# A weight ring of nine double slots and one spare slot in place of nineteen single slots

## The chip, the core and the metric

The kernel runs on one core of a Trainium2 chip. The metric is the device time of the program in microseconds (us); below it stands as the median of three runs. Float32 is used throughout.

## What is computed

A batch of one, T = 256 tokens, width D = 1024, goes through three layers. Layers 0 and 1 have a modulation from a condition vector, layer 2 has none:

```python
cond = silu(c)
for layer in range(2):                              # layers 0 and 1
    shift1, scale1, gate1, shift2, scale2, gate2 = split(cond @ ada_w[layer] + ada_b[layer], 6)
    h = rms(x, norm1_w[layer]) * (1 + scale1) + shift1
    y = even_mixer(h) if layer == 0 else odd_mixer(h)
    x = x + gate1 * y
    h = rms(x, norm2_w[layer]) * (1 + scale2) + shift2
    x = x + gate2 * hier_moe(h, w1, w3, w2)
h = rms(x, attn_norm_2); x = x + second_mixer(h)    # layer 2
x = x + hier_moe(rms(x, ffn_norm_2), w_gate, w_up, w_down)
return rms(x, final_norm_2)
```

The even mixer is a sliding-window attention beside a gated linear attention, the odd mixer a causal attention of 8 heads, the second one a sparse attention (compressed, selected and window branches) beside a linear recurrence, with gates that merge the two. Each mixer multiplies `h` by a wide input matrix and its result by an output matrix of 1024 x 1024. The MoE picks one of 4 groups and 2 of its 8 experts for each token; an expert is `(silu(t @ w1[e]) * (t @ w3[e])) @ w2[e]` with 512 hidden columns. So each of the 32 experts of a layer has three matrices of 2 MB (1024 x 512 twice, 512 x 1024 once), 192 MB a layer.

## The kernel before

All work is issued by one Python class, `Net`; the order of every engine's instructions is the order in which its methods emit them.

**The ring.** Big weights and the large buffers of the mixers share one pool of `RING` = 19 slots of 128 partitions x 2048 float32 (1 MB each, 8192 bytes a partition). `plan` (line 185) appends a transfer to a list: a key, the function that gives destination and source, and the shape. All of a program's transfers are planned at the start, in the order of their use: even mixer, MoE 0, odd mixer, MoE 1, second mixer, MoE 2. `pump` (line 188) takes transfers from the head of the list as long as the count `free` is above `reserve`, takes a slot of the ring for each and issues it on SyncE's queue (line 194). The count is kept in Python: it says how many slots the program order allows; on the chip SyncE waits at an issue until the slot's last readers are through. `get` returns a transfer that is issued, `done` gives its slot back and calls `release`, which raises `free` and pumps. `slot` takes a slot for a mixer's own buffer; `want` asks for one as soon as one is free; `reserve` keeps slots back for mixers' buffers that come later. For layer 2 a pool `extra` of two more slots, in space that the mixers have left, is used first (`more`).

**Mixers.** `plan_cols` (line 567) plans a slab of columns of an input matrix: 512 columns as two transfers of 1 MB (4 of 8 row groups each, 2048 bytes in a row), narrower slabs as one. `plan_rows` (line 574) plans half of an output matrix as two transfers of 512 columns. `plan_mod` (line 306) plans half of a modulation vector's matrix as two transfers with rows of 4 KB. Each chunk of two row groups of a slab is split into a rounded part and a rest by ScalarE, VectorE and GpSimd (`prep`, lines 461 to 463) into one of the mixer's split buffers `wbufs` (four slots; five in the second mixer, the fifth outside the ring); `prep` keeps at most one chunk fewer ready than there are buffers. `slab` then issues the matmuls of a chunk, each as three passes of the parts. The mixers' stages are interleaved by `weave`, a list of generators with written estimates of their times; beside them the modulation vectors are computed (`mods`, line 314) at places given by the lists `EVEN` and its like. A mixer ends with `out_last` (line 520), which takes `hT` (one slot, the turned tokens for the router) and `hs` (two slots, the tokens in two parts for the gather); `hs` stays through the MoE.

**MoE.** The 32 experts are handled in 16 pairs (`moe`, line 1791). A pair's tokens are gathered by matmuls into `xg`; `up` (line 1844) makes the gate pass and the up pass, `turn` transposes, `down` (line 1887) makes the down pass, `combine` adds the pair before into `x`. A pass alternates the two experts: each writes its 64 rows of the same result. The gate matrices of a pair are four transfers of 1 MB: `plan_moe` (line 1600) cuts every expert's matrix in halves, in the order expert 0 lower half, expert 1 lower half, expert 0 upper, expert 1 upper; each has rows of 8192 bytes a partition. `up` gives two slots back after its fourth row group and two at its end, `down` likewise after each half. The last pair's down matrices go in four slots of 256 columns of both experts (`down_last`, line 1910), so that the output can begin early. After pair 5 (`LATE`) an extra step serves tokens beyond an expert's 64 places. The numbers at the end of `moe`'s calls in `body` (line 2020; 8, 14, 0) are the slots that the last pair keeps back for the next mixer.

All matmuls of weights are at line 258 (`mm`), transposes at 268 (`tr`). Small operands are loaded on ScalarE's queue, `x` on SyncE's.

Of the kernel before, what the change touches and what calls it, by code (L numbers as in the profile page):

```python
# [9 lines left out]
FT = mybir.dt.float32  # L10
FR = mybir.dt.float32r
# [8 lines left out]
P = 128  # L20
# [9 lines left out]
RING = 19  # L30
# [92 lines left out]
class Net:  # L123
    def __init__(self, tc, ctx, A, out):
# [4 lines left out]
        self.ring = pool("ring", RING)  # L129
        self.ps = pool("ps", 8, space=PSUM)  # L130
# [35 lines left out]
    def outputs(self, c, key="out"):  # L166
        def use():
            s = self.slot(FR)
            self.o += [s[:, T * c * i:T * c * i + T * c].rearrange("p (c t) -> p c t", c=c) for i in range(SLOT // T // c)]
            self.flag((key, len(self.o)))  # L170
        self.want(use)
# [11 lines left out]
    def pump(self):  # L183
        while self.queue and (self.more or self.free > self.reserve):
            key, parts, (a, b) = self.queue.pop(0)
            if self.more:
                t = self.more.pop().tile([P, SLOT], FT, name="more", tag="more")
                self.mine.add(key)
            else:
                self.free -= 1  # L190
                t = self.ring.tile([P, SLOT], FT, name="slot", tag="slot")
# [122 lines left out]
    def mods(self, l, v, hs):  # L314
        p = self.psum()
        for h in hs:
            for j in range(2):
                w = self.get(("ada", l, v, h, j))
                for k in range(2):
                    for n in range(2):  # L320
                        q = slice(64 * n + 32 * k, 64 * n + 32 * k + 32)
                        self.mm(p[q], self.condz[:, 4 * h + 2 * j + k, 31 - v:63 - v], w[:, k, 512 * n:512 * n + 512],
                                h == hs[0] and not j, h == hs[-1] and j == 1)
                self.done(("ada", l, v, h, j))
# [98 lines left out]
    def begin_mixer(self, turned=None, mid=None):  # L423
# [4 lines left out]
        self.hh, self.hl = (self.slot(FR).rearrange("p (k q) -> p k q", k=KC) for i in range(2))  # L428
# [91 lines left out]
    def out_last(self, act, gate):  # L520
# [3 lines left out]
        self.hT = self.slot().rearrange("p (k q) -> p k q", k=KC)  # L524
        self.hs = [self.slot(FR).rearrange("p (t k q) -> p t k q", t=NT, k=KC) for i in range(2)]
# [41 lines left out]
    def plan_cols(self, key, w, c0, n):  # L567
        src = w.rearrange("(p k) n -> p k n", k=KC)[:, :, c0:c0 + n]
        m = KC if n * KC <= SLOT else 4
        for i in range(KC // m):  # L570
            self.plan((key, i), lambda t, i=i: [(t, src[:, m * i:m * i + m])], [m, n])
        self.chunks[key] = [((key, k // m), k % m, k % m == m - 2) for k in range(0, KC, 2)]

    def plan_rows(self, key, w, grouped=False):
        for i in range(2):
            ws = w[:, 512 * i:512 * i + 512]
            if grouped:
                src = ws.rearrange("(g r d) n -> g d r n", g=2, d=64)
                self.plan((key, i), lambda t, src=src: [(t[64 * g:64 * g + 64], src[g]) for g in range(2)], [4, 512])
            else:  # L580
                src = ws.rearrange("(k p) n -> p k n", p=P)
                self.plan((key, i), lambda t, src=src: [(t, src)], [4, 512])
        self.chunks[key] = [((key, i), k, k == 2) for i in range(2) for k in (0, 2)]
# [107 lines left out]
    def gla(self, g, q):  # L691
# [116 lines left out]
        self.release(4, reserve=3)  # L808
# [83 lines left out]
    def even(self, coeffs):  # L892
        nc = self.nc
        with self.tc.tile_pool(name="even", bufs=1, reuse_waits="tile") as g:
            setup = self.bias_setup(g)
            self.setup(lambda: next(setup))
            self.reserve = 10
# [8 lines left out]
            self.weights(["e_qa", "e_ka", "e_qb", "e_vb", "e_rb", "e_oa", "e_ob"], [self.slot(FR) for i in range(4)])  # L906
# [4 lines left out]
            bias, sc = (self.slot().rearrange("p (h s) -> p h s", h=8) for i in range(2))  # L911
            q = [self.slot() for i in range(2)]
# [31 lines left out]
            def stream():  # L944
                yield from self.slab_tm(512, s_qa)

                def use_att():
                    s = self.slot()
                    self.att, self.ob = s[:, :1024], s[:, 1024:]
                    self.flag("att", 0.7)  # L950

                def use_vb():
                    s = self.slot()
# [4 lines left out]
                self.want(use_vb)  # L958
# [1115 lines left out]
```

## Time and profile before

| | |
|---|---|
| median of three runs | 2072.07 us (2068.1 to 2073.53) |
| the profiled execution's own time | 2067.69 us |
| its span | 2065.9 us |
| mean granted TensorE clock | 0.974 |
| PE (matmul) busy | 1897.2 us, 92% |
| PEld (weight load) / DVE / ACT / POOL busy | 49% / 40% / 22% / 15% |
| moved by DMA | 725.29 MB, mean 351 GB/s |
| expert weights `slot<-moe_w` | 376 transfers of 1024 KB, 19.8 us from issue to landing |

Times are in us from the span's start. A row such as `ps<-slot,xg` names the written tile and the read ones; SPq is SyncE's queue of transfers. PEclk is the granted TensorE clock as a share of its full speed. Engines wait for each other and for transfers by semaphores; "<-" in brackets names what ended a wait. PE's matmuls follow each other in a pipeline, so a busy PE can be one that moves slowly through its queue.

### The profile page before, as it was taken

What the parts mean: (1) busy time and instruction counts of PE and PEld (TensorE: products, weight loads), DVE (VectorE), ACT (ScalarE), POOL (GpSimd) and SP (SyncE); (2) the same over time, 40 slices, a digit from 0 to 9 for tenths busy, and PEclk for the clock granted to TensorE, in tenths of its full rate; (3) what the DMA queues carried; (4) which work ended last, traced back from release to release, by engine and by line L of the source; (5) the groups of instructions that cost most, each with busy time, mean ns of one, the idle gap of its engine ahead of it and who ended that gap; (6) DMA issues with size and microseconds to landing.
All of it is one profiled execution on the core that took longest, in us unless ns stands there. A gap on an engine that the chain in (4) does not pass through costs nothing.

```text
span 2065.9 us, 25147 instructions
## 1 busy us (share of the span) xinstructions
PE 1897.2 (92%) x10032; PEld 1022.1 (49%) x10032; DVE 822.9 (40%) x1553; ACT 458.3 (22%) x838; POOL 309.8 (15%) x245
## 2 busy tenths in 40 slices
PE   6898999998989989999999889998899999999987
PEld 3655444343333657544433334586788443344333
DVE  3666433232322657623322222467666323222222
ACT  1424211111110443311111111254543111111111
POOL 1331000000000424000000000242443000000000
PEclk8998999999999999999999999999999999999999
DMA  8796999999999956799999999931357999999997
GB/s 314 274 312 251 375 422 421 420 421 422 421 420 405 367 211 242 303 401 421 421 421 421 421 421 421 342 106 42 131 191 268 379 421 421 420 421 421 421 421 287
DMA packets 157541, 725.29 MB, mean 351 GB/s; under 512 B 25305, under 2 KB 43087, under 8 KB 85225
## 3 DMA queue, kind: packets, MB, share of 16 engines
q1 hardware_dynamic: 139216, 716.84, 86.4%
q10 hardware_dynamic: 18201, 6.76, 1.3%
q8 instruction: 82, 1.34, 0.3%
q14 instruction: 42, 0.34, 0.0%
HBM read 722.48 MB, written 1.07 MB: 350 GB/s over the span
## 4 chain that ended last, share of the span: by engine, by line
DMA 23%; PE 19%; DVE 3%; issue 3%; ACT 2%; ACTq 0%; POOL 0%; POOLq 0%; SPq 0%; DVEq 0%
PE ps L258 18%; DMA slot<-moe_w 8%; DMA slot<-w_gate 5%; DMA slot<-w_up 4%; DMA slot<-w_down 2%; DMA more<-w_down 2%; DMA more<-w_up 2%; PE ps L268 1%; DVE slot L1287 1%; ACT slot L1275 1%; DMA slot<-w_in 0%; ACT slot L461 0%; DVE slot L462 0%; DVE hh L1861 0%; DVE wx L462 0%
## 5 line engine op out<-in xcount | busy, mean ns | idle before, releaser
L258 PE MATMUL ps<-slot,xg 128*64 128x512 f32 x2952 | 700.2, 599 | 47.5 <-DMA slot<-moe_w 34.3
L258 PEld LDWEIGHTS ps<-slot,xg 128*64 128x64 f32 x2952 | 225.0, 138 | 490.2 <-issue 381.2
L258 PE MATMUL ps<-slot 128*128 128x256 f32 (+8 forms) x2230 | 370.2, 327 | 11.5 <-DVE slot L462 9.0
L258 PE MATMUL ps<-slot,ht 128*64 128x512 f32 (+1 forms) x1592 | 341.7, 570 | 4.9 <-ACT ht L249 4.9
L258 PEld LDWEIGHTS ps<-slot 128*128 128x128 f32 (+3 forms) x2230 | 300.0, 186 | 72.2 <-issue 16.0
L1861 DVE SCALAR_TENSOR_TENSOR hh<-sg,ws,ps 128x512 f32<-128x512 f32 x48 | 54.3, 1130 | 603.6 <-PE ps L258 349.1
L258 PEld LDWEIGHTS ps<-slot,ht 128*64 128x64 f32 x1592 | 113.8, 137 | 198.1 <-issue 183.2
L1882 POOL TENSOR_TENSOR yl<-sg,yh 128x512 fp32r<-128x512 f32 (+1 forms) x68 | 82.4, 1211 | 862.5 <-ACT yh L1881 862.5
L463 POOL TENSOR_TENSOR slot<-slot 128x512 fp32r<-128x512 f32 (+2 forms) x108 | 163.5, 1531 | 279.5 <-ACT slot L461 247.3
L1908 DVE TENSOR_TENSOR x<-x,ps 128x512 f32<-128x512 f32 x180 | 113.6, 680 | 43.7 <-PE ps L258 41.5
L462 DVE TENSOR_TENSOR slot<-slot 128x512 fp32r<-128x512 f32 (+2 forms) x108 | 105.7, 992 | 57.3 <-ACT slot L461 54.6
L258 PEld LDWEIGHTS ps<-u,slot 128*128 128x128 f32 x864 | 105.6, 195 | 23.4 <-issue 17.0
L461 ACT CAST slot<-slot 128x1024 fp32r<-128x1024 f32 (+2 forms) x108 | 106.5, 1020 | 46.4 <-PE ps L258 24.8
L258 PE MATMUL ps<-u,slot 128*128 128x256 f32 (+1 forms) x864 | 111.0, 287 | 3.5 <-DVEq L1743 3.5
L1880 DVE TENSOR_TENSOR sg<-ps,ga 128x512 f32<-128x512 f32 (+1 forms) x68 | 44.9, 660 | 166.1 <-PE ps L258 155.8
L1857 ACT ACTIVATE sg<-ps 128x512 f32<-128x512 f32 x48 | 28.7, 597 | 325.7 <-PE ps L258 325.7
L1881 ACT CAST yh<-sg 128x512 fp32r<-128x512 f32 (+1 forms) x68 | 40.3, 593 | 251.7 <-DVE sg L1880 251.7
L258 PE MATMUL ps<-yh,pg 128*128 128x512 f32 (+1 forms) x204 | 85.5, 421 | 0.7 <-ACT yh L1881 0.7
L249 ACT COPY ht<-ps 128x512 f32<-128x512 f32 x48 | 28.1, 585 | 252.1 <-PE ps L268 251.9
L258 PE MATMUL ps<-yl,pg 128*128 128x512 f32 (+1 forms) x204 | 78.8, 389 | 4.3 <-POOL yl L1882 4.0
L399 ACT ACTIVATE xg<-ps,cf 128x256 f32<-128x256 f32 (+1 forms) x72 | 39.0, 542 | 172.6 <-PE ps L258 172.6
L1933 POOL TENSOR_TENSOR slot<-x,rows 128x512 f32<-128x512 f32 x2 | 2.6, 1276 | 460.2 <-DVE x L1929 460.2
(333 smaller groups left out, 1555.0 us busy)
## 6 DMA issues: line engine op xcount, KB each, us to landing
slot<-moe_w SPq DMA_DIRECT2D x376, 1024.0 KB, 19.8
slot<-w_gate SPq DMA_DIRECT2D x59, 1024.0 KB, 19.8
slot<-w_down SPq DMA_DIRECT2D x55, 1024.0 KB, 19.8
slot<-w_up SPq DMA_DIRECT2D x54, 1024.0 KB, 19.8
slot<-ada_w SPq DMA_DIRECT2D x48, 1024.0 KB, 9.0
slot<-w_in SPq DMA_DIRECT2D x20, 1024.0 KB, 7.4
slot<-odd_w_in SPq DMA_DIRECT2D x12, 1024.0 KB, 17.0
more<-w_up SPq DMA_DIRECT2D x10, 1024.0 KB, 16.1
```

The costliest lines, as they stand in the source:

```text
L249: self.nc.scalar.copy(out, in_)
L258: self.nc.tensor.matmul(out, lhsT=lhsT, rhs=rhs, start=start, stop=stop)
L399: self.nc.scalar.activation(out, p, AF.Identity, scale=a, bias=nb[:, k:k + 1])
L461: nc.scalar.copy(wh, src)
L462: nc.vector.tensor_sub(wl[:, 0], src[:, 0], wh[:, 0].bitcast(FT))
L463: nc.gpsimd.tensor_sub(wl[:, 1], src[:, 1], wh[:, 1].bitcast(FT))
L1857: nc.scalar.activation(sg, ps, AF.Silu)
L1861: nc.vector.scalar_tensor_tensor(ha.rearrange("s k p -> s p k"), st["sg", p].rearrange("s (p k) -> s p k", k=4), st["ws", p], ps.rearrange ...
L1880: nc.vector.tensor_mul(y, ps, self.ga[:, sl])
L1881: nc.scalar.copy(yh, y)
L1882: nc.gpsimd.tensor_sub(yl, y, yh.bitcast(FT))
L1908: nc.vector.tensor_add(self.x[:, t, sl], self.x[:, t, sl], ps)
```

## The change

The ring becomes nine double slots of 128 x 4096 float32 (2 MB each) and a pool `spare` of one single slot; together as many bytes as the 19 slots.

- An expert's gate, up or down matrix is one transfer of 2 MB with rows of 16384 bytes a partition, in one double slot. The order is expert 0, expert 1. Only the last pair of a layer has its gate and up matrices in two parts of 1 MB each (into one double) and its down matrices as two doubles of four parts of 512 KB. `up` and `down` give their two doubles back after the whole pass.
- A modulation half is one transfer of 2 MB, a 512-column slab one transfer of 2 MB, an output half one double filled by two or four transfers.
- Mixers' buffers are taken in pairs (`slots`, the two halves of a double): the turned input, the split buffers (two doubles; in the second mixer four buffers in place of five, the fifth being used for `q8`), bias and scores, and so on. Attention's and the value slab's buffers share a double, as do the two outputs. `hT`, the odd mixer's values, a buffer of the second mixer and the final output take the spare slot.
- The counts given to `release` and the reserves are restated in doubles (6 becomes 3, 10 becomes 5, the slots kept for the next mixer 8 and 14 become 4 and 6). `extra` is one double.

```diff
-RING = 19
+RING = 9
...
         self.ring = pool("ring", RING)
+        self.sp = pool("spare")
...
-    def slot(self, dtype=FT):
+    def slots(self, dtype=FT):
         assert self.free > 0
         self.free -= 1
         self.reserve = max(0, self.reserve - 1)
-        return self.ring.tile([P, SLOT], dtype, name="slot", tag="slot")
+        t = self.ring.tile([P, 2 * SLOT], dtype, name="slot", tag="slot")
+        return [t[:, :SLOT], t[:, SLOT:]]
+
+    def spare(self):
+        return self.sp.tile([P, SLOT], FT, name="spare", tag="spare")
...
-        for j in range(2):
-            self.plan(("ada", l, v, h, j), lambda t, j=j: [(t, src[:, 2 * j:2 * j + 2])], [2, D])
+        self.plan(("ada", l, v, h), lambda t: [(t, src)], [4, D])
...
-        self.hT = self.slot().rearrange("p (k q) -> p k q", k=KC)
-        self.hs = [self.slot(FR).rearrange("p (t k q) -> p t k q", t=NT, k=KC) for i in range(2)]
+        self.hT = self.spare().rearrange("p (k q) -> p k q", k=KC)
+        self.hs = [x.rearrange("p (t k q) -> p t k q", t=NT, k=KC) for x in self.slots(FR)]
...
-        m = KC if n * KC <= SLOT else 4
-        for i in range(KC // m):
-            self.plan((key, i), lambda t, i=i: [(t, src[:, m * i:m * i + m])], [m, n])
-        self.chunks[key] = [((key, k // m), k % m, k % m == m - 2) for k in range(0, KC, 2)]
+        self.plan(key, lambda t: [(t, src)], [KC, n])
+        self.chunks[key] = [(key, k, k == KC - 2) for k in range(0, KC, 2)]
...
             self.weights(["n_kv", "n_kw", "n_q", "h_f", "h_q", "h_i", "h_g", ("mg", 0), ("mg", 1), ("mg", 2), ("mg", 3),
-                          "brn", "brh", ("so", 0), ("so", 1)], [self.slot(FR) for i in range(4)] + [wx])
+                          "brn", "brh", ("so", 0), ("so", 1)], self.slots(FR) + self.slots(FR))
...
+        k2 = lambda w, e, k: w[e].rearrange("(p k) n -> p k n", k=k)
         for p in range(E // 2):
+            last = p == E // 2 - 1
             for nm, w in (("g", w1), ("u", w3)):
-                for i in range(4):
-                    src = w[2 * p + i % 2].rearrange("(p k) n -> p k n", k=KC)[:, i // 2 * 4:i // 2 * 4 + 4]
-                    self.plan((l, nm, p, i), lambda t, src=src: [(t, src)], [4, 512])
...
+                for i in range(2):
+                    src = k2(w, 2 * p + i, KC)
+                    self.plan((l, nm, p, i), lambda t, src=src, last=last: [(t[:, 4 * j:4 * j + 4], src[:, 4 * j:4 * j + 4])
+                                                                 for j in range(2)] if last else [(t, src)], [KC, 512])
+            for i in range(2):
+                if last:
+                    src = [k2(w2, 2 * p + j, 4) for j in range(2)]
+                    self.plan((l, "d", p, i), lambda t, i=i, src=src: [
+                        (t[:, 8 * h + 4 * j:8 * h + 4 * j + 4], src[j][:, :, 512 * i + 256 * h:512 * i + 256 * h + 256])
+                        for h in range(2) for j in range(2)], [16, 256])
+                else:
+                    src = k2(w2, 2 * p + i, 4)
+                    self.plan((l, "d", p, i), lambda t, src=src: [(t, src)], [4, D])
...
-                    if k % 4 == 3:
+                    if k == KC - 1:
                         self.done(*keys)
```

## Rows read from the trace of the kernel before

**Rows 1.** The page's 40 slices: DMA busy share in tenths, GB/s moved.
```profile
DMA  8796999999999956799999999931357999999997
GB/s 314 274 312 251 375 422 421 420 421 422 421 420 405 367 211 242 303 401 421 421 421 421 421 421 421 342 106 42 131 191 268 379 421 421 420 421 421 421 421 287
```

**Rows 2.** Windows over the MoE layers: from:to, length, busy (count) PE PEld DVE ACT POOL, PEclk, DMA, GB/s.
```profile
240.00:655.00 415.00, 391.59 (x1882) 167.29 (x1876) 118.58 (x187) 52.70 (x91) 38.25 (x30) 0.99 1.01 418
865.00:1300.00 435.00, 410.38 (x1956) 173.95 (x1954) 121.09 (x191) 55.08 (x95) 38.25 (x30) 0.99 1.01 418
1620.00:2040.00 420.00, 397.83 (x1914) 167.67 (x1910) 108.42 (x188) 50.16 (x92) 0.00 (x0) 1.00 1.01 421
```

**Rows 3.** Chain of waits, second half of layer 1 and the end: start, us, what.
```profile
1028.05 19.83 DMA slot<-moe_w
...
1160.37 19.80 DMA slot<-moe_w
...
2019.54 20.54 DMA slot<-w_up
2040.09 4.10 issue
```

**Rows 4.** Timeline of a pair in layer 0, PE: start, us, operation, count.
```profile
305.86 13.90 PE L258 MATMUL ps<-slot,xg 128*64 128x512 f32 x64
...
319.69 4.04 PE L258 MATMUL ps<-u,slot 128*128 128x256 f32 x32
...
326.18 7.09 PE L258 MATMUL ps<-slot,ht 128*64 128x512 f32 x32
```

**Rows 5.** Windows with rows of 1, 2, 4 and 8 KB prevailing.
```profile
662.00:670.00 8.00, 6.71 (x32) 2.44 (x28) 2.38 (x3) 0.00 (x0) 0.00 (x0) 1.00 1.08 345
1323.00:1332.00 9.00, 7.03 (x28) 6.87 (x29) 7.95 (x10) 3.88 (x7) 4.32 (x6) 0.81 1.05 386
70.00:78.00 8.00, 4.35 (x30) 4.15 (x30) 7.89 (x11) 4.81 (x7) 4.60 (x4) 0.90 1.03 409
926.00:966.00 40.00, 39.83 (x204) 17.83 (x202) 14.22 (x22) 5.76 (x10) 2.56 (x2) 1.00 1.01 421
```

**Rows 6.** The page's DMA queues: kind, packets, MB, share of 16 engines.
```profile
q1 hardware_dynamic: 139216, 716.84, 86.4%
...
q8 instruction: 82, 1.34, 0.3%
```

**Rows 7.** Timeline of layer 0's start, PE and SyncE's queue.
```profile
223.80 8.43 PE L258 MATMUL ps<-slot,xg 128*64 128x512 f32 x32
228.82 33.83 SPq L194 DMA_DIRECT2D slot<-moe_w  x16
...
235.93 7.09 PE L258 MATMUL ps<-slot,xg 128*64 128x512 f32 x32
...
254.79 9.61 PE L258 MATMUL ps<-slot,xg 128*64 128x512 f32 x44
```

**Rows 8.** Windows at the starts of layers 0 and 1.
```profile
228.60:231.20 2.60, 2.60 (x14) 0.84 (x12) 0.00 (x0) 0.00 (x0) 0.00 (x0) 1.00 0.54 117
235.00:300.00 65.00, 64.37 (x331) 28.61 (x331) 19.31 (x32) 10.59 (x19) 5.10 (x4) 1.00 0.99 404
875.00:940.00 65.00, 64.37 (x334) 28.64 (x332) 19.62 (x32) 9.41 (x17) 5.09 (x4) 1.00 0.99 405
```

**Rows 9.** Timeline in the even mixer, 104 to 135 us, PE and ACT.
```profile
107.26 1.92 PE L258 MATMUL ps<-slot,condz 128*32 128x512 f32 x16
...
113.08 2.00 ACT L461 CAST slot<-slot 128x1024 fp32r<-128x1024 f32 x2 [7.76 <-DMA slot<-even_w_in]
...
117.37 4.82 PE L258 MATMUL ps<-slot 128*128 128x512 f32 x23
```

**Rows 10.** The kernel's start: a timeline row of PE, the window over it.
```profile
33.60 1.06 PE L258 MATMUL ps<-slot,condz 128*32 128x512 f32 x8 [3.22 <-DMA slot<-ada_w]
...
0.00:34.00 34.00, 18.04 (x94) 9.61 (x98) 5.93 (x12) 3.94 (x10) 3.25 (x9) 1.00 0.87 303
```

More of the change, by code (lines that the diff above doesn't have):

```diff
@@ L167, in use @@
         def use():
-            s = self.slot(FR)
-            self.o += [s[:, T * c * i:T * c * i + T * c].rearrange("p (c t) -> p c t", c=c) for i in range(SLOT // T // c)]
-            self.flag((key, len(self.o)))
+            for s in self.slots(FR):
+                self.o += [s[:, T * c * i:T * c * i + T * c].rearrange("p (c t) -> p c t", c=c) for i in range(SLOT // T // c)]
+                self.flag((key, len(self.o)))
         self.want(use)
@@ L190, in pump @@
                 self.free -= 1
-                t = self.ring.tile([P, SLOT], FT, name="slot", tag="slot")
+                t = self.ring.tile([P, 2 * SLOT], FT, name="slot", tag="slot")
             v = t[:, :a * b].rearrange("p (k n) -> p k n", k=a)
@@ L427, in begin_mixer @@
             turned = self.transpose_x(self.x_rstd(4), mid, 3)
-        self.hh, self.hl = (self.slot(FR).rearrange("p (k q) -> p k q", k=KC) for i in range(2))
+        self.hh, self.hl = (x.rearrange("p (k q) -> p k q", k=KC) for x in self.slots(FR))
         for k0, p in zip(range(0, KC, 2), turned):
@@ L807, in gla @@
         self.flag("ob", 1.5)
-        self.release(4, reserve=3)
+        self.release(2, reserve=1)
     def swa(self, g, bias, sc):
@@ L896, in even @@
             self.setup(lambda: next(setup))
-            self.reserve = 10
+            self.reserve = 5
             next(setup)
@@ L905, in even @@
             self.norm_coeffs(0, 6, 0, 1)
-            self.weights(["e_qa", "e_ka", "e_qb", "e_vb", "e_rb", "e_oa", "e_ob"], [self.slot(FR) for i in range(4)])
+            self.weights(["e_qa", "e_ka", "e_qb", "e_vb", "e_rb", "e_oa", "e_ob"], self.slots(FR) + self.slots(FR))
             self.warm(2)
@@ L910, in even @@
             nc.gpsimd.tensor_scalar(self.nw[:, 0:1], self.nw[:, 0:1], 128 ** -0.5, None, op0=OP.mult)
-            bias, sc = (self.slot().rearrange("p (h s) -> p h s", h=8) for i in range(2))
-            q = [self.slot() for i in range(2)]
+            bias, sc = (x.rearrange("p (h s) -> p h s", h=8) for x in self.slots())
+            q = self.slots()
             self.o = []
@@ L983, in even @@
                        stream())
[L984 removed]
+        self.release(3)
     def plan_odd(self):
@@ L1005, in odd @@
             self.weights([("o", x) for x in (2, 0, 4, 3, 1, 5)] + [("oo", 0), ("oo", 1)],
-                         [self.slot(FR) for i in range(4)])
+                         self.slots(FR) + self.slots(FR))
             self.begin_mixer(mid=self.prep)
-            sa = [self.slot() for i in range(2)]
+            sa = self.slots()
             qT, kT = ([x[:, 1024 * i:1024 * i + 1024].rearrange("p (h t) -> p h t", h=4) for x in sa] for i in range(2))
@@ L1459, in hgrn @@
         self.flag("hg", 1.5)
-        self.release(5, reserve=2)
+        self.release(2, reserve=1)
     def second(self, coeffs):
@@ L1950, in moe @@
                 if last:
-                    self.reserve += max(0, slots - 2)
+                    self.reserve += max(0, slots - 1)
                     if l == 2:
-                        fo = self.slot().rearrange("p (t d) -> p t d", t=NT)
+                        fo = self.spare().rearrange("p (t d) -> p t d", t=NT)
                 else:
@@ L1973, in moe @@
                         if p == NP - 3:
-                            self.release(2, reserve=min(2, slots))
+                            self.release(1, reserve=min(1, slots))
                     elif due:
```

110 lines of the change are left out of this document (50 added, 60 removed).

## The prediction

> **What bounds the kernel now.** I read the 40 slices of the page first [rows 1]: three long stretches run at 420 to 422 GB/s with the DMA share at 9, and between them lie three valleys. The stretches are the three MoE layers, the valleys the three mixers. The windows over the layers say the same: 418, 418 and 421 GB/s, PE busy for 392 of 415 us, 410 of 435 and 398 of 420 [rows 2]. PE looks nearly as full as the DMA, so the chain of waits decides: in the second half of layer 1 it is eight transfers of expert weights one behind the other (1028.05 is the first, 1160.37 the last), and at the end of layer 2 the last `up` matrix lands at 2040.1 [rows 3]. A pair's own need on PE, read where PE does not starve: 13.9 us for the gate and up passes, 7.1 us for down, half of a 4.0 us gather, about 3 us of turns and combines [rows 4], some 26 us. Its 12 MB (12.58e6 bytes) take 29.9 us at 421 GB/s. So a layer begins on a reserve of loaded slots, uses it up by 4 us a pair, and from then on ends when the stream ends. A byte that comes earlier, or an idle us of the queue, is passed on to the end; only what loads while the ring stands full in a mixer is free.
>
> **Term 1, the rows: -17.8 us.** The expert matrices become 128 rows of 16384 bytes, two rows of 8192 in one. What a row costs beyond its bytes is read from four windows in which one row length prevails [rows 5]: 16 engines at 345 GB/s with 1024-byte rows are 47.5 ns a row, 386 with 2048 are 84.9 ns, 409 with 4096 are 160.2 ns, 421 with 8192 are 311.3 ns. Each doubling of the bytes leaves a fixed part (twice the shorter less the longer): 10.1, 9.6 and 9.1 ns. With 9.1 a 16384-byte row takes 613.5 ns, which is 427 GB/s. A 2 MB matrix has 8 such rows per engine, so 0.073 us less than now. 45 pairs (the last of each layer stays in 8192-byte parts) have 270 matrices; the first 8, 8 and 9 of the layers fill the ring beside the mixers, where the queue runs dry afterwards anyway. 245 x 0.073 = 17.8 us. From above, 10.1 ns would give 19.8. From below, the instruction queue already moves 16384-byte packets: 82 of them in 0.3% of 16 engines' span (99 us) [rows 6], about 1.2 us each against my 0.61. They go elsewhere than the weights and share their engine with them, so I don't take that as their price, but the trace has no weights row of this length: down to no gain at all I hold open.
>
> The fixed part of 9 to 10 ns, the same for rows of 1 to 8 KB, is what the rows show [rows 5]. The Trainium skill (DMA: Bandwidth & Descriptors, section "Why small descriptors are slow") gives a fixed 3 cycles per packet; at the 850 MHz fabric of its section "Where 436 GB/s comes from" that is 3.5 ns, and as an estimate from that page the term would be 245 x 8 x 3.5 ns = 6.9 us instead of 17.8. The measured fixed part is near three times that, so the sum goes by the rows.
>
> **Term 2, the start of each layer: +17 us.** Bytes of SBUF stay the same, but with hs taken the MoE ring has 8 doubles, 16 MB, where it had 17 slots (layer 2: 18 for 19); and a slot comes back only after the whole pass over a pair's gate (or up, or down), 4 MB at once, where 2 MB came back after half of it. Layer 0 [rows 7]: the first pass runs 223.8 to 232.2, now returning slots at its middle (SP issues at 228.82), the up pass ends at 243.0, down at 254.8. Now the queue is already short here: 117 GB/s from 228.6 to 231.2, which shows 2.4 us from issue to flow, and 404 from 235 to 300 [rows 8]; with 421 as full, 1.9 and 2.6 us are lost, and 1 us of ragged ends, 5.5 in all. After: the fill is over at about 228.6 as well (the mixer's split buffers come free in pairs, later, for 1 MB less). Return at 232.2, flow at 234.6: 6.0 us dry. 4 MB last 9.8 us, to 244.4; return at 243.0, flow at 245.4: 1.0 dry. Then to 255.2, return 254.8, flow 257.2: 2.0 dry. From there returns outrun the stream. 9.0 dry against 5.5, and 1 MB fewer loaded (2.5 us): 6.0 us. Layer 1 has the same shape and about the same loss now (405 GB/s from 875 to 940 [rows 8]); layer 2 I put at 5. Together 17. Lower bound 7.5, the missing 1 MB alone; upper 24, if the first passes wait as well.
>
> **Term 3, the even mixer: +4 us.** Around 100 us its ring streams four modulation matrices of 2 MB among the slabs. Now ACT waits 7.76 us for the first half of `e_rb` and splits it at 113.1; the slab's matmuls begin near 119.5, behind the end of the slab before it in the row at 117.37 [rows 9], so there is slack. After: three doubles stream beside the mixer's six. The matrix ahead of `e_rb` lands at about 115.7 (two transfers of 2 MB, 5.1 us each by the 409 GB/s row, behind issues at 103.5 and 108). `e_rb` can be issued when the second modulation is done with its double, 107.26 + 1.92 = 109.2; as one transfer of 2 KB rows it takes 5.4 us and lands at 121.2, 8 us later than its first half now. Its split adds 2.4, so 123.6 against 119.5: PE stops for 4 us, and ACT, which waits in order in front of the split, holds up the copy of the value slab queued behind it. Bounds: 0, if PE is late there anyway, and 12, if the doubles for attention and outputs are held from their allocation on, not from their first write, so that two stream.
>
> **Smaller terms.** Start of the kernel, -1: PE waits 3.22 us for the last modulation matrix at 33.6, in a stretch that moves only 303 GB/s [rows 10]. Four transfers instead of eight can bring that forward; PE then has its transposes to 26 and three passes of 1.93, so 2.9 us at most. Against it the first slab is one transfer, and its second MB is 2.7 us. Odd and second mixer, +1 (0 to 6): the split works on four buffers for five in the second one, three chunks ahead, and whole slabs load behind one another; two doubles cover a 10 us slab against 7.8 us of load, but ACT and DVE are in the way there. Last pair, +1: the transfers come as expert 0 lower, upper, expert 1 lower, upper, so the first half of the pass needs the third MB and not the second; 3.5 us of PE against 2.5 of stream leave 1.0 behind the landing at 2040.1 [rows 3]. Fewer waits and issues on SP and PE: nothing, the stream hides them; it is the stream itself where they would show.
>
> **Sum.** -17.8 + 17 + 4 - 1 + 1 + 1 = +4.2. The profiled execution took 2067.7 us (span 2065.9 and 1.8 around it): 2071.9. The median of the runs shown is 4.4 above it, and the forecast is for that: 2076. About 0.3%, 6.2 us, is what can be told from no change here, so this counts as the same. Its own range is 2070 to 2082.
>
> **Rivals.**
> *The gain stays* (25%). The dry spells at the layers' starts are there already, and if the new lumps fall into the same spells, only the missing MB counts (7.5), and `e_rb` comes in time: -17.8 + 7.5 + 0 - 1 + 1 + 1 = -9.3, 2063. For it: 5.5 us are lost there now [rows 8]. Against: the first return must come before 16 MB have landed, and the pass ends 3.6 us after.
> *The mixers' rings stall* (26%, slower). Mechanism: with doubles a mixer streams two at a time; place: `e_rb` in the even mixer, and then the output weights behind it; it decides once `e_rb` lands after about 119. With two doubles it is issued at about 116, lands near 126, and 4 becomes 10; 3 more in the second mixer with its ready chunks cut to three: 2085. For it: ACT waits for this very transfer now [rows 9]. Against: the outputs' double is not written before 150.
> *The row costs little* (5%). If only 3.5 of the 9.1 ns are per row and the rest grows with length, term 1 is -6.9, and the sum +15: 2087. This is the rule named under term 1; three pairs of row lengths with a steady 9 to 10 ns speak against it.
> *It does not do what it says* (4%): 16384-byte rows go out as two of 8192, or no faster, term 1 is nothing: +22, 2094.
>
> **Chances.** The forecast has 40%: 30 within 0.3%, 8 slower, 2 faster. The gain stays: 22 faster, 3 within. Stalls: 21 slower, 5 within. The two on the row: 9 slower. Together 24% faster, 38% within, 38% slower. The range takes terms 1 and 2 at their favourable and the mixers at their bad ends: 2058 to 2094.
>
> **What would show it.** Term 1: full windows at about 427 GB/s, packets of q1 fewer by 34,560. Term 2: dry windows of some 6 us behind the first gate pass of each layer, then two short ones. Term 3: the first split of `e_rb` near 121, a PE gap behind it. The forecast is wrong if the full windows stay at 421, if the layers' starts run full, or if the valleys grow by more than 10 us.

## The result: 1.0% slower, and the profile after

| | before | after |
|---|---|---|
| median | 2072.57 us (4 runs, 2068.1 to 2073.53) | 2093.53 us (4 runs, 2088.9 to 2096.39) |
| the profiled execution / its span | 2067.69 / 2065.9 us | 2096.39 / 2094.6 us |
| mean granted clock | 0.974 | 0.962 |

The ratio is 1.0103, with a 95% interval of 1.0079 to 1.0127, so +21 us, between +16 and +26. The two profiled executions lie 28.7 us apart, the one before being faster than its four runs and the one after the slowest of its four; the places of the loss are read from them, and the sums are to be taken with that in mind. Between the first gate pass and the last down pass of each layer, by the trace (us):

| stretch | before | after | more |
|---|---|---|---|
| start and even mixer, to layer 0's first gate pass | 223.8 | 239.0 | +15.2 |
| layer 0, to its last down pass | 455.8 | 459.5 | +3.7 |
| odd mixer | 181.3 | 181.5 | +0.2 |
| layer 1 | 456.8 | 461.6 | +4.8 |
| second mixer | 292.2 | 296.1 | +3.9 |
| layer 2 | 445.6 | 446.8 | +1.2 |
| end | 10.4 | 10.1 | -0.3 |

In these two profiles more than half is lost before the first expert is touched. The 40 slices of the page after (as [rows 1]) say the same: the plateaus rise from 421 to 427 or 428 GB/s, and in the first valley slices 2, 3 and 5 move 190, 233 and 293 GB/s where 274, 312 and 375 stood (slice 4 has 330 for 251).

```profile
DMA  9568799999999957799999999831247899999997
GB/s 330 190 233 330 293 412 428 428 426 429 427 428 415 346 167 262 281 396 427 428 427 428 427 428 424 293 110 70 81 167 282 362 429 427 427 427 427 427 428 280
```

The rows of the windows (from:to, length, busy us and count of PE, PEld, DVE, ACT, POOL, granted clock, DMA share, GB/s) through the middle of each layer, after; they answer to the full window of [rows 5] with its 421:

```profile
330.00:630.00 300.00, 279.03 (x1323) 118.60 (x1320) 83.90 (x129) 37.23 (x65) 25.48 (x20) 0.98 1.01 427
960.00:1260.00 300.00, 279.43 (x1310) 116.62 (x1305) 84.59 (x129) 36.89 (x63) 28.04 (x22) 0.98 1.01 427
1700.00:2000.00 300.00, 282.24 (x1340) 118.18 (x1338) 79.01 (x136) 34.85 (x63) 0.00 (x0) 0.99 1.01 427
```

And the queue's row of the page, which answers to [rows 6]: 39,600 packets fewer. 34,560 of them are the halved weights rows; the other 5,040 are 16 small packets for each of the 315 transfers that are gone (697 to 382).

```profile
q1 hardware_dynamic: 99616, 716.82, 83.7%
```

The starts of the layers, 76 us from each first gate pass, first before, then after (there with the first dry spell of layer 0 ahead):

```profile
224.00:300.00 76.00, 73.96 (x366) 31.64 (x366) 23.89 (x50) 12.03 (x21) 5.10 (x4) 0.98 0.96 391
861.00:937.00 76.00, 73.95 (x364) 31.62 (x366) 23.52 (x48) 12.34 (x21) 5.09 (x4) 0.98 0.99 404
1610.00:1686.00 76.00, 75.37 (x384) 32.26 (x386) 20.97 (x47) 11.44 (x23) 0.00 (x0) 1.00 0.95 393
```

```profile
245.00:251.00 6.00, 4.58 (x20) 1.49 (x16) 1.31 (x4) 0.99 (x2) 0.00 (x0) 1.00 0.41 109
239.00:315.00 76.00, 73.95 (x365) 31.70 (x366) 23.50 (x49) 12.35 (x21) 5.09 (x4) 0.98 0.92 378
...
880.00:956.00 76.00, 73.95 (x365) 31.64 (x366) 23.42 (x48) 12.43 (x21) 5.09 (x4) 0.98 0.92 378
1638.00:1714.00 76.00, 75.37 (x384) 32.27 (x382) 20.75 (x47) 11.44 (x23) 0.00 (x0) 1.00 0.91 384
```

What is short of the full rate in them is 5.4, 3.1 and 5.1 us before ((421 - 391)/421 x 76, and so on), 8.7, 8.7 and 7.7 us after: 11.5 us more. PE's busy time is the same in all pairs of windows: a layer starts on what is loaded, and the loss shows only when the stream ends.

In the even mixer the timeline of ACT shows where it waits (the bracket: idle time before, and what ended it). Before, the wait for the last input slab `e_rb` was 7.76 us [rows 9]; after, it is 18.69 us, and a second one stands at 156, for the output weights:

```profile
125.10 1.99 ACT L465 CAST slot<-slot 128x1024 fp32r<-128x1024 f32 x2 [18.69 <-DMA slot<-even_w_in]
126.99 0.58 ACT L254 COPY slot<-ps 128x512 f32<-128x512 f32 x1
127.47 1.04 ACT L465 CAST slot<-slot 128x1024 fp32r<-128x1024 f32 x1
...
156.14 2.00 ACT L465 CAST slot<-slot 128x1024 fp32r<-128x1024 f32 x2 [6.14 <-DMA slot<-even_w_out]
```

The copy at 126.99 is half of the value slab, held up behind the split. VectorE copies the other half at 129.80, behind its own parts of the split, and that copy is what PE waits for (5.96 us) before it starts the linear attention's state. The output weights are not issued before that attention is done on PE: SyncE's queue waits 26.1 us for PE there, to 148.2. SyncE's queue and PE, after:

```profile
110.79 0.55 SPq L199 DMA_DIRECT2D slot<-even_w_in  x1
115.51 6.55 SPq L199 DMA_DIRECT2D slot<-ada_w  x2
148.22 2.63 SPq L199 DMA_DIRECT2D slot<-even_w_out  x4
```

```profile
113.53 1.92 PE L263 MATMUL ps<-slot,condz 128*32 128x512 f32 x16 [1.21 <-DMA slot<-ada_w]
...
119.72 1.92 PE L263 MATMUL ps<-slot,condz 128*32 128x512 f32 x16 [1.30 <-DMA slot<-ada_w]
121.57 3.01 PE L263 MATMUL ps<-slot 128*128 128x512 f32 x12
130.55 3.35 PE L263 MATMUL ps<-slot 64*128 64x256 f32 x11 [5.96 <-DVE slot L256]
...
135.54 3.97 PE L263 MATMUL ps<-slot 128*128 128x512 f32 x12
139.44 0.59 PE L263 MATMUL ps<-st,slot 64*64 64x128 f32 x2
```

Before, the same transfers went out at 117.5, and the matmuls of 135.54 took 2.24 us for 3.97 (`plan` and `pump` stand at lines 180 and 183 of that kernel, not where the text on it has them):

```profile
108.57 4.51 SPq L194 DMA_DIRECT2D slot<-ada_w  x4
117.50 3.45 SPq L194 DMA_DIRECT2D slot<-even_w_out  x4
```

```profile
122.99 2.24 PE L258 MATMUL ps<-slot 128*128 128x512 f32 x12
125.16 0.43 PE L258 MATMUL ps<-st,slot 64*64 64x128 f32 x2
```

Where the mixer's 15 us arise shows when PE's matmuls are set side by side, each against the same one in the trace before:

| PE's matmul | before | after | late by |
|---|---|---|---|
| a modulation | 87.55 | 86.54 | -1.0 |
| the next modulation, behind a wait of 1.9 us at 95 | 101.60 | 103.14 | +1.5 |
| the first slab matmul behind the two waits for `ada_w` | 117.37 | 121.57 | +4.2 |
| the first of the linear attention's state | 120.41 | 130.55 | +10.1 |
| the first `st,slot`, twelve slab matmuls on | 125.16 | 139.44 | +14.3 |
| a transpose after the first splits of the output weights | 153.43 | 166.76 | +13.3 |
| layer 0's first gate pass | 223.80 | 239.0 | +15.2 |

So before the output weights are even issued, PE is as late, within a microsecond, as it is at the first gate pass. The stop of 6.0 us and 4.2 us of slower matmuls right behind it are two thirds; ACT's wait for the output weights at 156 adds nothing to PE's lateness here. Meanwhile the stream stands dry: the windows 95 to 100 and 140 to 150 us, first before, then after:

```profile
95.00:100.00 5.00, 5.00 (x39) 3.55 (x38) 4.50 (x13) 1.17 (x2) 0.00 (x0) 1.00 1.02 412
140.00:150.00 10.00, 9.21 (x52) 5.59 (x52) 9.21 (x15) 2.62 (x4) 8.88 (x7) 1.00 0.89 337
```

```profile
95.00:100.00 5.00, 4.60 (x14) 2.39 (x14) 2.81 (x9) 1.17 (x2) 0.00 (x0) 0.66 0.01 2
140.00:150.00 10.00, 10.00 (x57) 5.93 (x57) 1.73 (x4) 1.69 (x3) 0.00 (x0) 1.00 0.04 6
```

### The profile page after: what moved, and what is told of

Read it like the earlier page. It is cut to its first block, busy times and chain, and to the rows that moved or that the text cites. A ratio compares the mean times of both kernels' runs of the same rounds, so it can differ in the third digit from the quotient of the medians.

```text
span 2094.6 us, 24431 instructions
## 1 busy us (share of the span) xinstructions
PE 1919.7 (92%) x10032; PEld 1035.0 (49%) x10032; DVE 821.8 (39%) x1553; ACT 458.5 (22%) x838; POOL 309.1 (15%) x245
## 5 line engine op out<-in xcount | busy, mean ns | idle before, releaser
L263 PE MATMUL ps<-slot,xg 128*64 128x512 f32 x2960 | 714.3, 608 | 44.6 <-DMA slot<-moe_w 31.9
L263 PEld LDWEIGHTS ps<-slot,xg 128*64 128x64 f32 x2960 | 234.2, 140 | 487.1 <-issue 403.4
L263 PE MATMUL ps<-slot 128*128 128x256 f32 (+5 forms) x2356 | 398.0, 331 | 17.9 <-DVE slot L466 7.3
L263 PEld LDWEIGHTS ps<-slot 128*128 128x128 f32 (+2 forms) x2356 | 325.9, 191 | 80.5 <-issue 15.9
L467 POOL TENSOR_TENSOR slot<-slot 128x512 fp32r<-128x512 f32 (+2 forms) x120 | 180.7, 1525 | 308.2 <-ACT slot L465 297.7
L466 DVE TENSOR_TENSOR slot<-slot 128x512 fp32r<-128x512 f32 (+2 forms) x120 | 118.0, 996 | 72.4 <-ACT slot L465 71.8
L465 ACT CAST slot<-slot 128x1024 fp32r<-128x1024 f32 (+2 forms) x120 | 118.3, 1019 | 68.4 <-PE ps L263 26.4
L263 PE MATMUL ps<-u,slot 128*128 128x256 f32 (+1 forms) x864 | 110.8, 287 | 3.5 <-DVEq L1748 3.5
L1861 ACT ACTIVATE sg<-ps 128x512 f32<-128x512 f32 x48 | 28.7, 597 | 328.2 <-PE ps L263 328.2
```

The costliest lines, as they stand in the source:

```text
L263: self.nc.tensor.matmul(out, lhsT=lhsT, rhs=rhs, start=start, stop=stop)
L465: nc.scalar.copy(wh, src)
L466: nc.vector.tensor_sub(wl[:, 0], src[:, 0], wh[:, 0].bitcast(FT))
L467: nc.gpsimd.tensor_sub(wl[:, 1], src[:, 1], wh[:, 1].bitcast(FT))
L1861: nc.scalar.activation(sg, ps, AF.Silu)
```

## Experiments

Below, "first pass" is the start of layer 0's first gate pass in a run's own profile, and ratios are to the kernel before, measured beside it. A single profile scatters: `before` and `e7` have the same even mixer and first passes at 223.8 and 227.0; after, `e1` and `e2` have the same one too and show 239.0, 234.9 and 233.9. First passes are one profile each, so less than about 5 us between two of them says little.

### What the long rows are worth, and what the whole pass costs

`e1_rows_8k` undoes the row length alone:

```diff
-                                                                 for j in range(2)] if last else [(t, src)], [KC, 512])
+                                                                 for j in range(2)], [KC, 512])
...
-                    self.plan((l, "d", p, i), lambda t, src=src: [(t, src)], [4, D])
+                    self.plan((l, "d", p, i), lambda t, src=src: [(t[:, 2 * j:2 * j + 2], src[:, 2 * j:2 * j + 2])
+                                                                  for j in range(2)], [4, D])
```

> The changed kernel with one thing undone: each 2 MB expert matrix goes as two transfers with rows of 8192 bytes into its double slot, in the order expert 0 lower, upper, expert 1 lower, upper; slots, returns and mixers stay. Theory A (the long row is worth 0.073 us a matrix, as term 1 has it): full windows fall from 427 to 421 GB/s and the time rises by 17.8 us from 2093.5 to 2111. Rival (the long rows give nothing that reaches the end, the layers are bound by when slots come back): 2093, within 4 us.

Measured: 2104.98 us, ratio 1.0159 (1.0142 to 1.0176). Its windows are back at 421 in all three layers:

```profile
330.00:630.00 300.00, 274.85 (x1306) 118.91 (x1306) 85.44 (x133) 37.82 (x65) 25.48 (x20) 0.99 1.01 421
960.00:1260.00 300.00, 278.12 (x1308) 114.39 (x1304) 84.75 (x129) 36.53 (x63) 28.02 (x22) 0.98 1.01 421
1700.00:2000.00 300.00, 282.52 (x1341) 117.23 (x1338) 77.28 (x133) 34.87 (x63) 0.00 (x0) 0.99 1.01 421
```

The rival, that the rate does not reach the end, falls: 11.5 us between the medians. Theory A's 17.8 lies within what the two intervals leave (3 to 20 us); by the windows a matrix takes 4.911 us for 4.981, and 245 of them 17.2 us. In the two profiles the three layers together differ by 13.9 us.

`e2_halves` keeps the short rows and gives back what the whole matrix took away: a double holds the same half of both experts.

```diff
+                    src = [k2(w, 2 * p + j, KC)[:, 4 * i:4 * i + 4] for j in range(2)]
+                    self.plan((l, nm, p, i), lambda t, src=src: [(t[:, 4 * j:4 * j + 4], src[j]) for j in range(2)], [KC, 512])
...
+                    key = (l, nm, p, k // 4)
...
-                    if k == KC - 1:
-                        self.done(*keys)
+                    if k % 4 == 3:
+                        self.done(key)
```

> Like the one before (rows of 8192 bytes, double slots), but a double holds the same half of both experts' matrices, so that 2 MB come back after half a pass, and the stream's order is that of the kernel before. Theory A (giving slots back only after a whole pass, and needing both whole matrices before a pass begins, costs some 3 us at each layer's start and 3 to 4 us at the ends of layers 0 and 1): 2111 - 9 - 9 = 2093, and PE ends a layer 10.5 us behind the landing of its last bytes as before, not 14. Rival (the grain of returning costs nothing, only the missing 1 MB does): same as the kernel with whole matrices in 8192-byte rows, 2111.

Measured: 2088.36 us, ratio 1.0085 (1.0066 to 1.0104), 16.6 us below the kernel with whole matrices in short rows. That is the price of the whole-pass grain, and it has two places. The starts, 76 us from each first gate pass, first `e1`, then `e2`, lose 20.6 and 11.7 us against 421 GB/s:

```profile
235.00:311.00 76.00, 73.95 (x372) 31.82 (x374) 24.24 (x50) 12.36 (x21) 5.10 (x4) 1.00 0.96 385
882.00:958.00 76.00, 73.95 (x372) 31.75 (x370) 24.15 (x50) 12.17 (x21) 5.10 (x4) 1.00 0.95 386
1640.00:1716.00 76.00, 75.37 (x384) 32.27 (x382) 20.82 (x47) 11.44 (x23) 0.00 (x0) 1.00 0.92 378
```

```profile
234.00:310.00 76.00, 73.97 (x372) 31.81 (x372) 24.26 (x50) 12.27 (x21) 5.10 (x4) 1.00 0.99 405
870.00:946.00 76.00, 73.96 (x364) 31.69 (x366) 23.19 (x49) 12.71 (x23) 5.10 (x4) 0.98 0.97 396
1621.00:1697.00 76.00, 75.39 (x384) 32.37 (x386) 21.02 (x48) 11.54 (x22) 0.00 (x0) 1.00 0.96 397
```

In `e2`'s profile the three layers take 454.9, 456.8 and 447.0 us, within 1.4 us of the kernel before; but that execution, at 2080.34 us, is the fastest of its four, 8 us under their median. The ends show in PE's timeline: the up pass of pair 14 in layer 0, which waits for its bytes, first before, then after:

```profile
632.59 3.65 PE L258 MATMUL ps<-slot,xg 128*64 128x512 f32 x14 [1.33 <-DMA slot<-moe_w]
```

```profile
647.84 7.08 PE L263 MATMUL ps<-slot,xg 128*64 128x512 f32 x30 [1.09 <-DMA slot<-moe_w]
```

With halves, half of a pass is left when the last bytes land (3.65 us, in `e2` too); with whole matrices both experts are needed for its first step, and 7.08 us are left. In layers 0 and 1 PE is the late one from there to the layer's end, so 3.4 us are lost in each.

### The even mixer: which transfer, and why

Four changes of the kernel after, one at a time.

`e3_out_late` asks for the outputs' double only after the last slab.

```diff
                 yield from self.mix(self.slab_fm(4, s_qb), 16, self.ev[1])
-                self.outputs(4)
...
                 yield from self.mix(self.slab_tm(512, s_rb), 8, self.ev[3])
+                self.outputs(4)
                 self.release()
```

> The changed kernel with the even mixer's output double asked for after the last slab's pass instead of before the value slab, so that one more double streams meanwhile. Theory A (two streaming doubles are too few there): the first split of the last input slab comes near 115 instead of 125.1, the first pass of layer 0 at about 231 instead of 239, time 2086. Rival B (the slab comes late because a slab is one transfer of 2 MB that must land whole): no more than 2 us gained, 2092.

Measured: 2091.55 us, ratio 1.0083 (1.0066 to 1.01). The split of `e_rb` comes at 123.4, first pass 234.5, as in `e1` and `e2` (splits at 123.8 and 122.9, first passes 234.9 and 233.9), whose mixer is that of the kernel after. Theory A's reading of it falls: the double is not held from the request. Requests are Python's counting; the buffer itself seems to be taken with its first write only.

`e4_cols_two` loads each slab by two transfers into the halves of its double.

```diff
-        self.plan(key, lambda t: [(t, src)], [KC, n])
+        m = KC if n * KC <= SLOT else 4
+        self.plan(key, lambda t: [(t[:, m * i:m * i + m], src[:, m * i:m * i + m]) for i in range(KC // m)], [KC, n])
```

> The changed kernel with each 512-column slab loaded as two transfers of 1 MB into the halves of its double (all three mixers). Rival B (whole transfers make the splits late): the first split of the even mixer's last slab comes 2.7 us earlier or more, and with the other slabs 8 us are gained, 2085. Theory A (the number of streaming doubles is what counts): 2092 to 2094, the issue of that slab stays at about 110.8 us.

Measured: 2090.79 us, ratio 1.0079 (1.0053 to 1.0104); the split at 121.8, first pass 231.9. PE's stop before the linear attention is 3.26 us, where it is 5.9 to 6.7 in after, `e1`, `e2` and `e3`. So about 3 us of that stop are the whole transfer; what reaches the first pass, 2 us or more, is within the scatter.

`e5_even_order` plans `e_rb` ahead of two modulation halves, and `e8_before_order` does so in the kernel before.

```diff
-EVEN = (1, 1, 4, 1, 1, 2, 2)
+EVEN = (1, 1, 2, 2, 2, 2, 2)
```

> The changed kernel with the even mixer's last input slab planned before two of the four modulation halves that stream ahead of it (EVEN is (1, 1, 2, 2, 2, 2, 2)). Theory A2 (with three streaming doubles the slab can't be issued until PE has used up two modulations, so its place in the stream makes it late): its first split comes near 114 us instead of 123 to 125, the output weights follow, the first pass of layer 0 starts 8 us earlier (228 instead of 236), time 2093.5 - 8 = 2085.5. Rival C (PE itself is late there, or the output weights, which come later anyway, set the end): the split comes earlier, but the first pass starts within 2 us of before, time 2092.

> The kernel before with the even mixer's order changed as in the first kernel of this group (last input slab ahead of two modulation halves). Control: theory A2 says that a ring of nineteen single slots holds 8 MB there and the order matters little: 2073 to 2075, first pass of layer 0 at 222 to 226 us. Rival (the order is better for any ring): the first pass at 219 or earlier, 2069.

Measured: 2091.1 us, ratio 1.0104 (1.0087 to 1.0121), and for the control 2072.98 us, 1.0014 (1.0003 to 1.0025), first pass 224.5. In `e5` the split comes at 113.9, as forecast, and nothing is gained: first pass 237.3. Rival C was right. With `e_rb` out of the way, what is late next are the output weights:

```profile
155.14 1.99 ACT L465 CAST slot<-slot 128x1024 fp32r<-128x1024 f32 x2 [4.51 <-DMA slot<-even_w_out]
159.81 1.04 ACT L465 CAST slot<-slot 128x1024 fp32r<-128x1024 f32 x1 [2.68 <-DMA slot<-even_w_out]
```

Their splits stand in ACT's order ahead of the sliding-window softmax, which begins at 168 there and at 157.5 in the kernel before. So `e9_oa_early` plans them right behind `e_rb`, with four modulation halves behind them, and `e11_before_oa_late` moves them back in the kernel before:

```diff
-EVEN = (1, 1, 4, 1, 1, 2, 2)
+EVEN = (1, 1, 2, 0, 4, 2, 2)
...
         cols("e_rb", 1792, 512)
+        self.plan_rows("e_oa", wo[:512], grouped=True)
         ada(*self.ev[3])
         ada(*self.ev[4])
-        self.plan_rows("e_oa", wo[:512], grouped=True)
```

```diff
         ada(*self.ev[4])
-        self.plan_rows("e_oa", wo[:512], grouped=True)
         ada(*self.ev[5])
+        self.plan_rows("e_oa", wo[:512], grouped=True)
```

> The changed kernel with only the even mixer's plan reordered: the first half of the output matrix (e_oa) is planned right behind the last input slab and four modulation halves behind it (EVEN is (1, 1, 2, 0, 4, 2, 2), their matmuls after that slab's pass). Theory A3 (what sets the mixer's end is that e_oa is issued at 147 us where the kernel before issued it at 117.5, and that ACT and DVE hold its splits in order ahead of the attention's softmax): e_oa is issued before 125 us, ACT no longer waits for it, the softmax's exponentials begin near 158 to 160 instead of 168, the first pass of layer 0 starts at 226 to 229 (239.0, 234.9, 233.9 and 234.5 in the four runs with the changed order), time 2085. Rival (the doubles make the mixer late wherever the transfers stand; the delayed modulations take over): first pass at 234 or later, 2092.

> The kernel before (nineteen single slots) with one thing moved: e_oa is planned behind the two modulation halves that follow it now (four more slots ahead of it). Theory A3: e_oa is issued some 20 us later than 117.5, near 140, ACT waits for it ahead of the softmax, and the loss of the changed kernel appears without any double slot: first pass of layer 0 at 230 to 234 instead of 224, time 2072 + 8 = 2080. Rival (the late output weights have slack): 224 to 226, 2072.

Measured: `e9` 2100.83 us, ratio 1.0141 (1.0118 to 1.0163), first pass 246.8: the worst of all. ACT no longer waits for the output weights, but PE does for the modulations that were moved behind them:

```profile
161.46 1.92 PE L263 MATMUL ps<-slot,condz 128*32 128x512 f32 x16 [1.81 <-DMA slot<-ada_w]
168.18 3.64 PE L263 MATMUL ps<-slot,condz 128*32 128x512 f32 x16 [3.95 <-DMA slot<-ada_w]
```

`e11`: 2072.45 us, ratio 1.0009 (0.9996 to 1.0022), first pass 225.5. Its output weights are issued 22 us later than before (139.7) and ACT does wait for them, yet their last split is only 5.1 us later (152.68 against 147.59) and the mixer 1.7. Theory A3, that this one transfer sets the end, falls in both directions.

`e12_before_hold` takes away bytes instead: the kernel before with one slot held through the even mixer.

```diff
+            self.held = self.slot()
+            nc.gpsimd.memset(self.held[:, :8], 0.0)
```

Its reserves are raised by one, and `hT` takes the held slot. Counted in the program's order, both rings then have 8 MB for transfers when the mixer begins, 6 once the attention's and value slab's buffers are taken and 4 with the outputs'; the kernel before has 9, 7 and 5.

> The kernel before with the slot of hT taken at the start of the even mixer and written once there, so that the mixer has eighteen single slots, the bytes that the nine doubles leave it (the spare slot stands empty until hT is written). Theory C (the missing 1 MB makes the even mixer late): the first split of the last input slab at 118 us or later instead of 113.1, first pass of layer 0 at 230 to 236, time 2080. Theory G (the grain does it: a transfer waits for two neighbouring megabytes to come free at once, and 2 MB for one use is the smallest step): 113 to 115, first pass at 224 to 227, time 2072 to 2075.

Measured: 2071.02 us, ratio 0.9994 (0.9982 to 1.0006), first pass 224.4. The split comes at 116.4, between the two theories, but the missing megabyte does not reach the end: it is not the cause.

What all of them have in common is seen in one window, 60 to 160 us:

| kernel | GB/s | granted clock | first pass |
|---|---|---|---|
| before | 290 | 0.94 | 223.8 |
| `e11` | 274 | 0.94 | 225.5 |
| `e7` (below) | 274 | 0.96 | 227.0 |
| `e12` | 269 | 0.96 | 224.4 |
| `e8` | 267 | 0.96 | 224.5 |
| `e10` (below) | 228 | 0.96 | 232.6 |
| `e6` (below) | 224 | 0.94 | 232.1 |
| `e4` | 214 | 0.95 | 231.9 |
| `e2` | 209 | 0.91 | 233.9 |
| `e3` | 205 | 0.93 | 234.5 |
| `e5` | 202 | 0.94 | 237.3 |
| `e1` | 201 | 0.90 | 234.9 |
| after | 198 | 0.91 | 239.0 |
| `e9` | 174 | 0.85 | 246.8 |

The rows of before, `e12` and after:

```profile
60.00:160.00 100.00, 86.34 (x528) 56.91 (x527) 64.48 (x130) 37.01 (x56) 33.94 (x24) 0.94 0.84 290
```

```profile
60.00:160.00 100.00, 86.09 (x527) 56.51 (x525) 65.20 (x130) 35.31 (x50) 33.94 (x24) 0.96 0.78 269
```

```profile
60.00:160.00 100.00, 84.79 (x489) 56.66 (x488) 55.10 (x106) 29.77 (x40) 28.98 (x21) 0.91 0.58 198
```

With single slots the mixer is fed 267 to 290 GB/s, with doubles 174 to 228, and by and large the less arrives the later it ends. The rate is cause and effect at once, since a mixer that waits gives nothing back; but `e12` has the same bytes in single slots and is fed 269. So it is the doubles that starve the mixer, and the planned order only chooses which transfer is the late one. How they do it is not shown. That a transfer waits until two megabytes are free at once is one reading; others are that the mixer's own buffers, taken in pairs, come free later (attention with the value slab, the two outputs), and that a 1 MB slab fills a double. None was tried by itself, since the mixers' transfers can't take halves of a double that come free one by one.

### The second mixer

`e7_before_split4`: the kernel before with four split buffers in the second mixer.

```diff
-                          "brn", "brh", ("so", 0), ("so", 1)], [self.slot(FR) for i in range(4)] + [wx])
+                          "brn", "brh", ("so", 0), ("so", 1)], [self.slot(FR) for i in range(4)])
```

> The kernel before with four split buffers instead of five in the second mixer, nothing else. Theory (this part of the change makes the second mixer's 2 to 5 us): the second mixer, from the end of layer 1's down pass to the first pass of layer 2, takes 294 to 297 us instead of 292.2, time 2073 + 3 = 2076. Rival (it is the ring of doubles there): 292, time 2073.

Measured: 2077.0 us, ratio 1.0032 (1.0011 to 1.0052), its second mixer 297.0 us. That speaks for the theory, but weakly: `e8`, which leaves this mixer alone, shows 294.5 in its profile, and the kernels with the changed second mixer 293.7 to 297.1. Its even mixer, which it does not touch, is 3.2 us late as well. How much of the 3.9 us the fifth buffer explains stays open.

### Putting the parts together

`e6_edges` has long rows in pairs 2 to 13, halves of both experts in pairs 0, 1 and 14, slabs in two transfers and the order of `e5`; `e10_all` is the same with the order of `e9`. With the edits of `e2`, `e4` and `e5` (or `e9`) shown above:

```diff
+HALF = (0, 1, 14, 15)
...
+                    if p in HALF:
+                        src = [k2(w, 2 * p + j, KC)[:, 4 * i:4 * i + 4] for j in range(2)]
...
+                    if p in HALF and k % 4 == 3:
+                        self.done(keys[k // 4])
+                    elif p not in HALF and k == KC - 1:
+                        self.done(*keys)
```

> Version put together from the parts: double slots and rows of 16384 bytes for the pairs 2 to 13 of each layer; pairs 0, 1 and 14 with the same half of both experts in a double, as the last one has too; the even mixer's order as in the run before; slabs as two transfers. Theory A2: 2090.8 (slabs in two) - 8 (order) - 16.6 (return after half a pass, now at the layers' edges only) + 4 (three more pairs in short rows) = 2070, same as or a little faster than the kernel before (2073). Rival (the whole-pass return costs in every pair, not at the edges): no gain from the edges, 2083.

> The version with long rows in pairs 2 to 13, half-pass returns at the layers' edges and slabs in two transfers, now with this plan of the even mixer. Theory A3: 2073.7 - 7 = 2067, faster than the kernel before (2071 to 2073) by 4 to 6 us. Rival: 2074.

Measured: 2073.69 us, ratio 1.0016 (1.0003 to 1.0029), and 2076.46 us, 1.002 (1.0007 to 1.0032). The edges give back nearly all of the 21 us, some 17 against `e5` (the slabs in two transfers, which `e6` has besides, are worth nothing that the medians of `e4` and `e5` could tell), so the whole-pass return costs at the layers' edges and hardly between them. Layer 0 takes 455.6 us in `e6`, layer 1 457.0, layer 2 441.4, and its first pass is still 8.3 us late. No version beat the kernel before.

## Why the prediction was off, step by step

The likeliest case, about the same time, did not come. What came is nearest in size to the rival in which the mixers' rings stall (2085). The time lies inside the stated range by half a microsecond, and that is luck: with the mixers at their bad ends (12 and 6) the prediction's own terms give 2089, and its upper end of 2094 is the price of the rival without any gain from the long rows, a gain that did come.

- **Start, -1:** right. Most instructions between 45 and 88 us come 0.9 to 1.0 us earlier.
- **Term 1, -17.8:** right. 16384-byte rows at 427 GB/s are 613.9 ns for the 613.5 that the fixed part of 9.1 ns gave [rows 5]; the term is 17.2 by the windows, and undoing it cost 11.5 between the medians, with 3 to 20 open. By the rule of the Trainium skill (DMA: Bandwidth & Descriptors, "Why small descriptors are slow"), 3 cycles a packet, the estimate of 6.9 us would have been 423.4 GB/s (a matrix 0.028 us shorter); the windows' 427 disagrees, so here the measurement decides.
- **Term 2, +17:** right in size. The windows lose 11.5 us more than before, and 1 MB fewer in each reserve (2.5 us each) makes it 19. The first dry spell after the gate pass is there (109 GB/s from 245 to 251). The missing megabyte was not tried by itself, but `e1`, with the old row length, leaves room for it: its layers take 23.6 us more than before, its starts lose 7.0 more and its ends some 8, and the other 8 or 9 stand against the term's 7.5.
- **Term 3, +4:** this step failed, in its price and not in its path. As it said, ACT's wait for `e_rb` held up the copies of the value slab and PE stopped behind them: the slab was issued at 110.8 where it had 109.2, its split began at 125.1 where it had 121.2, and PE stopped for 6.0 us where it had 4. It counted the stop and nothing around it. Two waits of PE for modulation matrices come before (2.5 us), the matmuls behind the stop run slower (4.2 us: 8.89 for 4.75, from the state's first matmul to the first `st,slot`), and in this profile a wait of 1.9 us at 95 us with slow matmuls behind it makes 2.5 more. In after, `e1`, `e2` and `e3` PE is 12.0 to 14.3 us late by the first `st,slot`, and 10.1 to 15.2 at the first gate pass. The rival looked for the rest in the output weights; they do go out 31 us later, but cost PE nothing until `e_rb` is moved ahead of them (`e5`). What argued against the rival, that the outputs' double is not written before 150, fits `e3`: asking for that double later changed nothing.
- **Last pair, +1:** mis-sized. It is the pass that first needs both whole matrices, in pair 14 as in 15: 3.4 us in layers 0 and 1, about 1 in layer 2.
- **Odd and second mixer, +1:** 0.2 and 3.9.

So the two large terms cancelled as forecast, and the sum was missed by 7 to 12 us in the even mixer (first pass 10 to 15 us late, where start and term 3 made 3), by some 7 at the layers' ends and by about 3 in the second mixer. That the mixer's 10 to 15 us come from the doubles is shown in so far as neither the bytes (`e12`), nor the order (`e5`, `e8`, `e9`, `e11`), nor the time of the request (`e3`) does it; which property of the doubles stays open.

## What to carry to other kernels

A larger transfer can be faster on the wire and still lose: the unit that is loaded becomes the unit that is given back and the unit that must be complete before work begins, so price the three separately, at the edges of each stage, where the reserve is used up. Where a ring feeds a stage with many different weights, look at the bytes that arrive in a window of it, not at one late transfer: moving that one earlier makes another late. Price a stop of PE with the slower matmuls behind it. An in-order engine that splits weights ahead of other work passes every late landing on to that work.

## What had not been expected

A stall is paid twice: where PE waits in the even mixer, the granted clock falls, and the matmuls behind the wait run slower. It was 0.74 from 120 to 140 us in the kernel after and 1.00 before; from 130 to 140, behind the stop of 6.0 us, it was 0.51, the lower of the two levels (1.2 of 2.4 GHz). First before, then after:

```profile
120.00:140.00 20.00, 20.00 (x120) 12.18 (x120) 10.13 (x31) 6.02 (x8) 2.60 (x3) 1.00 1.04 283
```

```profile
120.00:140.00 20.00, 14.04 (x63) 9.42 (x55) 9.42 (x26) 3.42 (x4) 4.68 (x3) 0.74 0.68 267
...
130.00:140.00 10.00, 9.45 (x35) 6.93 (x35) 5.72 (x22) 0.00 (x0) 0.89 (x1) 0.51 0.32 129
```

Each transfer carries 16 packets of 4 bytes beside its rows, of 9 to 10 ns each: 315 transfers fewer were 5,040 packets fewer. By that they are some 3 us of the 16 engines' time over the whole program; the part of it that lies in the layers is within the 427 GB/s.
